# Nine norm factors by way of DRAM in place of TensorE products, in a two-layer hybrid decoder

## The chip, the cores and the metric

The kernel runs on one NeuronCore of a Trainium2 chip. The metric is the device time of one execution in microseconds (us), the median of several runs; lower is better. Beside the runs stands one profiled execution, whose trace gives every instruction's engine, start and duration.

The engines are TensorE (PE in the profile; PEld is its weight loading), VectorE (DVE), ScalarE (ACT), GpSimd (POOL) and SyncE (SP). Each takes its instructions strictly in the order in which the program has them, so an instruction that waits holds back all behind it on its engine. SP issues the weight loads; POOL issues the small transfers of this kernel.

## The reference, cut to what matters

Two layers on 256 positions of width 2048, batch 1, all in float32. The first layer mixes positions by a state-space model (SSD), the second by forgetting attention (FoX). Every branch begins and ends with an RMS norm.

```
def rmsnorm(x, w):
    y = x * rsqrt(mean(x * x, axis=-1) + EPS)        # one factor for each position
    return y * w

# end of the state-space mixer: 8 groups of 512 channels, each with a norm of its own
y  = y.reshape(b, l, 4096) * silu(z)
yg = y.reshape(b, l, 8, 512)
yg = yg * rsqrt(mean(yg * yg, axis=-1, keepdims=True) + EPS)
y  = yg.reshape(b, l, 4096) * norm_w
return y @ w_out

# the attention layer's first norm
proj = rmsnorm(h, norm_mix_pre[1]) @ fox_w_in       # q, k, v and the forget gates
```

A position's factor multiplies all channels of that position. The kernel holds activations with channels on the 128 partitions and the 256 positions along the free dimension (a tile is 128 x 256), so a factor has to be present on all 128 partitions, as a row of 256 numbers repeated 128 times.

## The kernel before

**Weights.** Every weight matrix is streamed once, in stages of up to 128 x 1024 numbers. For each stage SP loads a tile `raw` (six buffers), ScalarE casts it to a high part `wh` in the fast float32r format (L204), and VectorE subtracts to get a low part `wl` (L209); both have four buffers. TensorE then makes three products for each 128 x 128 block: weight high by activation high (L266), high by low (L267), low by high (L268). Stages are prepared two ahead of the one in use. A unit is one call of `unit`: a set of output columns over the whole contraction, here mostly 4 blocks of 128 columns in 8 stages of 24 products.

**Side work.** What else has to be done (transposes, small products, exponentials, scalings) stands in a queue of little tasks, `bg`; `unit` takes one task (sometimes two) from it after each stage's products. This sets the order of the program's text. A scheduler then orders each engine's instructions by its own estimate of when their operands will be ready, so an instruction can end up ahead of its place in the text. Where the text says `tc.issue_after` (and the helper `paced`, which ties an operation to the last low part), that order is kept.

**Norm factors.** `rstd_small` turns the sums of squares (a 128 x 256 tile of partial sums) into factors: four narrow products on TensorE (L349) put positions on partitions, VectorE makes mean plus epsilon (`ms`, L352), POOL takes the power -1/2 (`rs`, L355). `rs` is 128 x 2: position on the partition, half of the sequence in the column. `rstd_wide` spreads it: VectorE splits `rs` into high and low (`rh`, `rl`; L360, L361), TensorE makes four products with the identity as moving operand and the factor as broadcast weights (L365), ScalarE copies the result out of PSUM (L369). It is called 18 times in all.

**State-space stage (about 125 to 525 us).** For group g there is an xs unit (its outputs go through the convolution `conv_silu` into four tiles `xg`), the core tasks `core_tasks(g)` (decay matrices `E`, transposes of `xg` at L977 into `xd`, products of `E` and `xd` at L1018, then y), a z unit (y times the gate, sums of squares into `ssp`), and the gate tasks: `gn1` makes the small factor, `gn2` spreads it into `grw` (one buffer), `gn3` scales the group's four y tiles (L1055). The tasks of group g's norm run beside the xs unit of group g + 2. The last two groups' scalings are `paced` and stand among the tasks of the out-projection (`last7`). `ab`, the broadcast of the decays from DRAM, and the clearing of three columns of `xr` for each convolution are POOL's other work here.

**FoX layer (about 1480 us on).** The V part is five units with positions on the output partitions, so it needs only the small factor (`rsm`). `mk_r(False, rsm)` makes it, and spreads it into `rwide` for the q and k units; `rq` is `rwide` times the attention scale.

Of the kernel before, what the change touches and what calls it, by code (L numbers as in the profile page):

```python
# [7 lines left out]
F32 = mybir.dt.float32  # L8
# [6 lines left out]
P = 128  # L15
# [6 lines left out]
NG = 8  # L22
# [41 lines left out]
def tile_trunk(ctx, tc, a, out):  # L64
    nc = tc.nc
    mult, add, sub, mx_, mn_ = ALU.mult, ALU.add, ALU.subtract, ALU.max, ALU.min
    V, A, G, PE = nc.vector, nc.scalar, nc.gpsimd, nc.tensor

    def pool(stack, name, bufs=1, **kw):
        return stack.enter_context(tc.tile_pool(name=name, bufs=bufs, **kw))  # L70
# [10 lines left out]
    gap = pool(ctx, "gap")  # L81
    psa = pool(ctx, "psa", bufs=6, space=PSUM)
    psm = pool(ctx, "psm", bufs=2, space=PSUM)

    cnt = [0]

    def nm(s):
        cnt[0] += 1
        return f"{s}_{cnt[0]}"
# [268 lines left out]
    def rstd_wide(rs, o):  # L358
# [10 lines left out]
            mark[0] = A.copy(out=o, in_=ps[:, :T])  # L369
        return ps[:, :T]  # L370

    def log1p_exp_neg_abs(v, new):
        ab = new()
        V.scalar_tensor_tensor(out=ab, in0=v, scalar=-1.0, in1=v, op0=mult, op1=mx_)
        e = new()
        A.activation(e, ab, AF.Exp, scale=-1.0)
        d = ab
        V.tensor_scalar(out=d, in0=e, scalar1=2.0, scalar2=None, op0=add)
        r = new()
        V.reciprocal(out=r, in_=d)  # L380
        s = new()
        V.tensor_tensor(out=s, in0=e, in1=r, op=mult)
        q = r
        V.tensor_tensor(out=q, in0=s, in1=s, op=mult)
        pl = ab
        V.tensor_scalar(out=pl, in0=q, scalar1=1.0 / 13, scalar2=None, op0=mult)
        for k in (11, 9, 7, 5, 3):
            V.scalar_tensor_tensor(out=pl, in0=pl, scalar=1.0 / k, in1=q, op0=add, op1=mult)
        o = e
        V.scalar_tensor_tensor(out=o, in0=pl, scalar=1.0, in1=s, op0=add, op1=mult)  # L390
        return o
# [26 lines left out]
    rwide = cp.tile([P, T], F32, name="rwide")  # L418
# [122 lines left out]
    def mk_r(half=True, small=None):  # L541
        r = []

        def f1():
            r.append(rstd_small(ssb, D))
            if small is not None:
                V.tensor_copy(out=small, in_=r[0])

        def f2():
            rstd_wide(r[0], rwide)  # L550
            if half:
                V.tensor_scalar(out=rwide2, in0=rwide, scalar1=0.5, scalar2=None, op0=mult)
        return f1, f2
# [268 lines left out]
    with ExitStack() as ys:  # L822
        yp = pool(ys, "yp", side="right")
        y = [yp.tile([P, T], F32, name=f"y{c}") for c in range(32)]
        with ExitStack() as st:
# [136 lines left out]
            def core_tasks(g, xg):  # L962
                S = {}
                for q in range(2):
                    h0 = 8 * g + 4 * q
                    ab = s3[0].tile([P, 4, T], F32, tag="ab", name=nm("ab"), bufs=2)
                    G.dma_start(
                        out=ab.rearrange("p a n -> p (a n)"),
                        in_=acd[h0:h0 + 4, :].rearrange("h n -> (h n)").partition_broadcast(P))
                    S[f"a{q}"] = ab  # L970

                def xpose():
                    xd = S["xd"] = s3[0].tile([P, 2, 512], F32, tag="xd", name=nm("xd"), bufs=2)
                    ps = [misc(), misc()]

                    def turned(j, c):
                        return PE.transpose(out=ps[j][:, c * P:(c + 1) * P],  # L977
                                            in_=xg[c][:, j * P:(j + 1) * P], identity=ident)
                    joined(lambda: turned(0, 3),
                           [lambda j=j, c=c: turned(j, c) for j in range(2) for c in range(4)  # L980
                            if (j, c) != (0, 3)])
                    for j in range(2):
                        V.tensor_tensor(
                            out=xd[:, j, :].rearrange("p (h d) -> p h d", d=64),
                            in0=ps[j].rearrange("p (h d) -> p h d", d=64),
                            in1=dtk[:, j, 8 * g:8 * g + 8].unsqueeze(2).broadcast_to((P, 8, 64)),
                            op=mult)

                def decay(q, half):
                    h0 = 8 * g + 4 * q  # L990
                    ab = S[f"a{q}"]
                    if half == 0:
                        S[f"E{q}"] = s3[0].tile([P, 4, 384], F32, tag="E", name=nm("E"), bufs=2)
                    E = S[f"E{q}"]
                    with after(low_a[0]):
                        for i in range(2 * half, 2 * half + 2):
                            for b, lo in ((0, 0), (1, P), (2, P)):
                                A.activation(E[:, i, b * P:(b + 1) * P], ab[:, i, lo:lo + P],
                                             AF.Relu, scale=-1.0,
                                             bias=bias3[:, b, h0 + i:h0 + i + 1])  # L1000

                def decay2(q):
                    E = S[f"E{q}"]
                    with after(low_a[0]):
                        A.activation(E, E, AF.Exp, scale=-1.0)
                    V.tensor_tensor(out=E, in0=E,
                                    in1=cbm[g].unsqueeze(1).broadcast_to((P, 4, 384)),
                                    op=mult)

                def ymm_of(q):  # L1010
                    E, xd = S[f"E{q}"], S["xd"]
                    ps = S[f"p{q}"] = misc()

                    def mm(pr, s, b):
                        i = 2 * pr + s
                        hl = 4 * q + i
                        o = ps[s * 64:(s + 1) * 64, pr * T:(pr + 1) * T]
                        return PE.matmul(o[:, b * P:], lhsT=xd[:, b, hl * 64:(hl + 1) * 64],  # L1018
                                         rhs=E[:, i, b * T:(T, 384)[b]], start=b == 0,
                                         stop=b == 1)  # L1020
                    return [lambda pr=pr, s=s, b=b: mm(pr, s, b)
                            for pr in range(2) for b in range(2) for s in range(2)]

                def ymm():
                    todo = ymm_of(1) + ymm_of(0)
                    joined(todo[0], todo[1:])

                def y_of(q):
                    for pr in range(2):
                        c = 2 * q + pr  # L1030
                        V.scalar_tensor_tensor(out=y[4 * g + c], in0=xg[c],
                                               scalar=col("ssd_d", 4 * g + c),
                                               in1=S[f"p{q}"][:, pr * T:(pr + 1) * T],
                                               op0=mult, op1=add)

                def ymm_y():
                    ymm()
                    y_of(1)

                return [lambda: decay(0, 0), lambda: decay(0, 1), xpose, lambda: decay2(0),  # L1040
                        lambda: decay(1, 0), lambda: decay(1, 1), lambda: decay2(1), noop, ymm_y,
                        lambda: y_of(0), noop]

            def gate_tasks(g, S):
                def gn1():
                    S["rs"] = rstd_small(S["ss"], 512)

                def gn2():
                    S["rw"] = yp.tile([P, T], F32, tag="grw", name=nm("grw"), bufs=1)
                    rstd_wide(S["rs"], S["rw"])  # L1050

                def gn3():
                    for c in range(4):
                        yc = y[4 * g + c]
                        last_v[0] = V.scalar_tensor_tensor(out=yc, in0=yc, scalar=col("ssd_norm", 4 * g + c),  # L1055
                                               in1=S["rw"], op0=mult, op1=mult)
                if g < NG - 2:
                    return [noop, gn1, gn2, gn3]
                late.append(lambda: paced(gn3))
                return [noop, gn1, gn2] if g < NG - 1 else [gn1, noop, gn2, noop]  # L1060

            xgs, late, later, last7 = {}, [], [], []
            zt = {}

            def z_a(t):
# [87 lines left out]
                bg.append(lambda c=c: ysplit(c))  # L1153
            left[0] = 0
            z_unit(NG - 1, 2)
        xq_s = ExitStack()
        xq = pool(xq_s, "xq", bufs=16)
        zp = pool(xq_s, "zp")
        for t in range(4):
            acc, yc, ss = later[t]  # L1160
# [98 lines left out]
    for u in range(1, 5):  # L1259
        unit(lambda k: nxt[k], both if u == 1 else ev_v(u), tok=True,  # L1260
             late=(lambda: (drain(), v1()), v2) if u == 1 else ())
        if u == 1:
            V.tensor_scalar(out=rq, in0=rwide, scalar1=float(FOXS), scalar2=None, op0=mult)
    bg.extend((f1, noop, f2, noop, f3))
    ots = {}
# [178 lines left out]
```

## Time and profile before

| | |
|---|---|
| median of 3 runs | 2704.6 us (2704.22 to 2705.89) |
| profiled execution, its own time | 2704.73 us |
| its span, first to last instruction | 2702.9 us |
| TensorE busy | 2696.0 us |
| VectorE busy | 1782.5 us |
| ScalarE busy | 1398.9 us |
| POOL busy | 46.8 us |
| mean granted TensorE clock | 1.000 |
| weight loads (queue of SP) | 504.54 MB |

The span is what the instructions cover; the profiled execution's own time is 1.8 us more. Busy TensorE does not mean that it is at its peak, since matmuls overlap: what one costs is seen from the distance between starts. A row of the order of time gives the start, the duration, engine, line, operation, output tiles and input tiles, how many instructions of the kind followed each other, and in brackets how long the engine was idle before and who ended that. A row of a group gives count, busy time, mean duration and the idle time ahead.

### The profile page before, as it was taken

The numbers are of one execution on the slowest core, as the hardware profiler recorded it, in microseconds if no ns is written. First come the engines' busy times: TensorE is split into PE (matmuls) and PEld (weight loads), VectorE is DVE, ScalarE is ACT, GpSimd is POOL, SyncE is SP. The second block draws the span as 40 slices with busy tenths as digits, with TensorE's granted clock in tenths as the row PEclk, the third lists the DMA queues.
The fourth block names the chain that finished last, engine by engine and source line by source line (L and its number), as shares of the span: only waits on it lengthen the run. The fifth ranks groups of instructions, "written<-read, shape, count | busy, mean of one in ns | idle before, by whom it ended". The sixth has DMA issues, their size and how long they took to land. (4 is left out here: it accounts for less than half of the span.)

```text
span 2702.9 us, 56196 instructions
## 1 busy us (share of the span) xinstructions
PE 2696.0 (100%) x23302; PEld 2680.0 (99%) x23302; DVE 1782.5 (66%) x2747; ACT 1398.9 (52%) x2156; POOL 46.8 (2%) x108
## 2 busy tenths in 40 slices
PE   9999999999999999999999999999999999999999
PEld 9999999999999999999999999999999999999999
DVE  8788888754966545666568656656865545656577
ACT  6577666554644444444446544455644444444455
POOL 0000000000000000000000000000000000000000
PEclk9999999999999999999999999999999999999999
DMA  7666666565666666666656676655766666666655
GB/s 267 190 203 203 189 196 189 162 213 174 195 203 195 195 195 193 192 176 208 199 162 208 180 223 184 178 160 171 205 203 194 195 195 192 193 180 209 195 165 171
DMA packets 262736, 520.42 MB, mean 193 GB/s; under 512 B 17440, under 2 KB 44224, under 8 KB 262480
## 3 DMA queue, kind: packets, MB, share of 16 engines
q1 hardware_dynamic: 258784, 504.54, 62.2%
q0 software_dynamic: 3552, 12.15, 1.4%
q8 instruction: 182, 2.98, 0.5%
q14 instruction: 74, 0.61, 0.1%
q10 hardware_dynamic: 144, 0.14, 0.0%
HBM read 514.58 MB, written 2.18 MB: 191 GB/s over the span
## 5 line engine op out<-in xcount | busy, mean ns | idle before, releaser
L209 DVE TENSOR_TENSOR wl<-raw,wh 128x1024 fp32r<-128x1024 f32 (+4 forms) x1020 | 1174.2, 1153 | 751.9 <-ACT wh L204 750.5
L204 ACT CAST wh<-raw 128x1024 fp32r<-128x1024 f32 (+4 forms) x1020 | 1014.2, 997 | 1116.6 <-PE acc L267 985.0
L267 PE MATMUL acc<-x,wh 128*128 128x256 f32 x5120 | 1392.0, 277 | 0.0
L268 PE MATMUL acc<-x,wl 128*128 128x256 f32 x5120 | 1365.4, 276 | 0.0
L266 PE MATMUL acc<-x,wh 128*128 128x256 f32 x5120 | 1356.6, 277 | 0.1
L267 PEld LDWEIGHTS acc<-x,wh 128*128 128x128 f32 x5120 | 961.0, 188 | 2.0 <-issue 1.9
L268 PEld LDWEIGHTS acc<-x,wl 128*128 128x128 f32 x5120 | 948.2, 188 | 0.8 <-issue 0.7
L266 PEld LDWEIGHTS acc<-x,wh 128*128 128x128 f32 x5120 | 936.2, 188 | 1.4 <-issue 0.9
L267 PE MATMUL acc<-a,wh 128*128 128x256 f32 x1408 | 388.1, 276 | 0.0
L266 PE MATMUL acc<-a,wh 128*128 128x256 f32 x1408 | 388.0, 276 | 0.0
L268 PE MATMUL acc<-a,wl 128*128 128x256 f32 x1408 | 385.4, 275 | 0.0
L267 PEld LDWEIGHTS acc<-a,wh 128*128 128x128 f32 x1408 | 264.4, 188 | 0.0
L266 PEld LDWEIGHTS acc<-a,wh 128*128 128x128 f32 x1408 | 264.2, 188 | 0.0
L268 PEld LDWEIGHTS acc<-a,wl 128*128 128x128 f32 x1408 | 263.5, 188 | 0.0
L266 PE MATMUL acc<-xb,wh 128*128 128x256 f32 x512 | 143.8, 281 | 1.1 <-DVE qk L296 1.1
L267 PE MATMUL acc<-xb,wh 128*128 128x256 f32 x512 | 141.4, 276 | 0.0
L268 PE MATMUL acc<-xb,wl 128*128 128x256 f32 x512 | 140.6, 276 | 0.0
L266 PEld LDWEIGHTS acc<-xb,wh 128*128 128x128 f32 x512 | 96.1, 188 | 1.7 <-DVE qk L296 1.5
L267 PEld LDWEIGHTS acc<-xb,wh 128*128 128x128 f32 x512 | 96.2, 188 | 0.2
L268 PEld LDWEIGHTS acc<-xb,wl 128*128 128x128 f32 x512 | 95.8, 188 | 0.2 <-issue 0.2
L914 DVE SCALAR_TENSOR_TENSOR g<-xr,vec,g 128x256 f32<-128x256 f32 x144 | 66.5, 481 | 8.2 <-ACT g L911 7.6
L266 PE MATMUL acc<-xq,wh 128*128 128x256 f32 x256 | 70.7, 276 | 0.0
(217 smaller groups left out, 1984.4 us busy)
## 6 DMA issues: line engine op xcount, KB each, us to landing
raw<-down SPq DMA_DIRECT2D x176, 512.0 KB, 3.9
raw<-ssd_in SPq DMA_DIRECT2D x144, 512.0 KB, 4.1
raw<-gate SPq DMA_DIRECT2D x128, 512.0 KB, 3.7
raw<-up SPq DMA_DIRECT2D x128, 512.0 KB, 3.6
raw<-fox_in SPq DMA_DIRECT2D x64, 512.0 KB, 4.0
raw<-gate SPq DMA_DIRECT2D x64, 384.0 KB, 3.2
raw<-up SPq DMA_DIRECT2D x64, 384.0 KB, 3.5
raw<-ssd_out SPq DMA_DIRECT2D x40, 512.0 KB, 4.4
```

What stands on the lines that cost most here:

```text
L204: low_a[0] = A.copy(out=wh[:, :kc * n], in_=raw[:, :kc * n])
L209: low[0] = V.tensor_tensor(out=wl[:, :kc * n], in0=raw[:, :kc * n], in1=wh.bitcast(F32)[:, :kc * n], op=sub)
L266: PE.matmul(o, lhsT=w, rhs=x[:, 0, :], start=st, stop=False)
L267: PE.matmul(o, lhsT=w, rhs=x[:, 1, :], start=False, stop=False)
L268: last = PE.matmul(o, lhsT=wl[:, c, t * P:(t + 1) * P], rhs=x[:, 0, :], start=False, stop=sp)
L914: V.scalar_tensor_tensor(out=c, in0=xr[:, k:k + T], scalar=col(f"conv_w{k}", cc), in1=c, op0=mult, op1=add)
```

## The change

A new pool of DRAM tiles and a new helper `rstd_sent` stand beside `rstd_wide`. The helper writes `rs` from the partitions into 256 consecutive numbers in DRAM, and reads them back to all 128 partitions; both transfers are issued by POOL. It takes the place of `rstd_wide` in the eight group norms and in the FoX layer's first norm. `gn2` is gone; `gn1` now does both steps. For the first six groups `gn3` is put into a list `scale` and called from a later place of the task queue, where the core tasks had a `noop`. The eighth group's scaling comes one task later. `rq` is written behind the last V unit in place of the second.

```
+    rp = pool(ctx, "rp", space=bass.MemoryType.DRAM)
...
+    def rstd_sent(rs, o):
+        d = rp.tile([2, P], F32, tag="rsd", name=nm("rsd"), bufs=2)
+        G.dma_start(out=d.rearrange("j p -> p j"), in_=rs)
+        G.dma_start(out=o, in_=d.rearrange("j p -> (j p)").partition_broadcast(P))
...
         def f2():
-            rstd_wide(r[0], rwide)
+            (rstd_wide if half else rstd_sent)(r[0], rwide)
...
-                        lambda: decay(1, 0), lambda: decay(1, 1), lambda: decay2(1), noop, ymm_y,
+                        lambda: decay(1, 0), lambda: decay(1, 1), lambda: decay2(1), scale_y, ymm_y,
...
                 def gn1():
-                    S["rs"] = rstd_small(S["ss"], 512)
-
-                def gn2():
                     S["rw"] = yp.tile([P, T], F32, tag="grw", name=nm("grw"), bufs=1)
-                    rstd_wide(S["rs"], S["rw"])
+                    rstd_sent(rstd_small(S["ss"], 512), S["rw"])
...
                 if g < NG - 2:
-                    return [noop, gn1, gn2, gn3]
+                    return [noop, gn1, lambda: scale.append(gn3), noop]
                 late.append(lambda: paced(gn3))
-                return [noop, gn1, gn2] if g < NG - 1 else [gn1, noop, gn2, noop]
+                return [noop, gn1, noop] if g < NG - 1 else [gn1, noop, noop, noop, noop]
+
+            def scale_y():
+                if scale:
+                    scale.popleft()()
...
-        if u == 1:
+        if u == 4:
             V.tensor_scalar(out=rq, in0=rwide, scalar1=float(FOXS), scalar2=None, op0=mult)
```

What the scheduler makes of it, on VectorE around the scaling of the fourth group. Before (`wl` are low parts, `ms` the mean plus epsilon, `y` with `grw` the scaling, `xr` the evacuation of the next unit's outputs):

```order
L352 TENSOR_SCALAR ms_4797<-mi_4794 128x2
L209 TENSOR_TENSOR wl_4845<-raw_4842,wh_4844 128x1024
L360 CAST rh_4832<-rs_4799 128x2
L361 TENSOR_TENSOR rl_4833<-rs_4799,rh_4832 128x2
L209 TENSOR_TENSOR wl_4879<-raw_4876,wh_4878 128x1024
L1055 SCALAR_TENSOR_TENSOR y_193<-y_193,vec,grw_4831 128x256
L1055 SCALAR_TENSOR_TENSOR y_194<-y_194,vec,grw_4831 128x256
L1055 SCALAR_TENSOR_TENSOR y_195<-y_195,vec,grw_4831 128x256
L1055 SCALAR_TENSOR_TENSOR y_196<-y_196,vec,grw_4831 128x256
L296 TENSOR_TENSOR xr_4906<-acc_4618,rwide 128x256
L209 TENSOR_TENSOR wl_4961<-raw_4958,wh_4960 128x1024
```

and the same place now:

```order
L353 TENSOR_SCALAR ms_4779<-mi_4776 128x2
L210 TENSOR_TENSOR wl_4819<-raw_4816,wh_4818 128x1024
L210 TENSOR_TENSOR wl_4849<-raw_4846,wh_4848 128x1024
L1058 SCALAR_TENSOR_TENSOR y_195<-y_195,vec,grw_4775 128x256
L1058 SCALAR_TENSOR_TENSOR y_196<-y_196,vec,grw_4775 128x256
L1058 SCALAR_TENSOR_TENSOR y_197<-y_197,vec,grw_4775 128x256
L1058 SCALAR_TENSOR_TENSOR y_198<-y_198,vec,grw_4775 128x256
L297 TENSOR_TENSOR xr_4876<-acc_4599,rwide 128x256
L210 TENSOR_TENSOR wl_4931<-raw_4928,wh_4930 128x1024
```

The two small operations are gone; the scaling stands where it stood, two low parts behind `ms`, though its call in the text is some eight stages later. It is the same for the other five of the first six groups; in the first three, evacuations and convolution steps stand between `ms` and the scaling as well. On POOL at the same place, before (`rs` is the power, `ab` the broadcast of decays):

```order
L908 MEMSET xr_4906 128x3
L908 MEMSET xr_4917 128x3
L355 TENSOR_TENSOR rs_4799<-ms_4797,mhalf 128x2
L908 MEMSET xr_4928 128x3
L967 DMA ab_5611<-acd 128x1024
L908 MEMSET xr_4939 128x3
```

and now:

```order
L914 MEMSET xr_4876 128x3
L973 DMA ab_4922<-acd 128x1024
L914 MEMSET xr_4887 128x3
L356 TENSOR_TENSOR rs_4781<-ms_4779,mhalf 128x2
L375 DMA rsd_4783<-rs_4781 128x2x1
L376 DMA grw_4775<-rsd_4783 128x256
L914 MEMSET xr_4898 128x3
L973 DMA ab_5574<-acd 128x1024
```

The two new transfers stand directly behind the power, ahead of the clearing of the next `xr`; the second cannot be issued before the first has landed. On TensorE the 36 products are gone, and some of the state-space stage's own products stand elsewhere among the weight products: the eight transposes of the third group 20 products earlier, of the fourth 38 later, of the fifth 12 earlier, of the sixth and seventh 10 later, and the first product of E and xd of the fifth group 18 earlier. SP's queue is the same row for row.

More of the change, by code (lines that the diff above doesn't have):

```diff
@@ L1057, in gate_tasks @@
                 if g < NG - 2:
-                    return [noop, gn1, gn2, gn3]
+                    return [noop, gn1, lambda: scale.append(gn3), noop]
                 late.append(lambda: paced(gn3))
-                return [noop, gn1, gn2] if g < NG - 1 else [gn1, noop, gn2, noop]
-            xgs, late, later, last7 = {}, [], [], []
+                return [noop, gn1, noop] if g < NG - 1 else [gn1, noop, noop, noop, noop]
+            def scale_y():
+                if scale:
+                    scale.popleft()()
+            xgs, late, later, last7, scale = {}, [], [], [], deque()
             zt = {}
@@ L1155, in tile_trunk @@
             z_unit(NG - 1, 2)
+            assert not scale
         xq_s = ExitStack()
```

## The prediction

> **What bounds the kernel now.** I read the page's busy shares first, then the costliest groups, then the order of time on TensorE around one of the products that go.
>
> ```profile
> PE 2696.0 (100%) x23302; PEld 2680.0 (99%) x23302; DVE 1782.5 (66%) x2747; ACT 1398.9 (52%) x2156; POOL 46.8 (2%) x108
> L209 DVE TENSOR_TENSOR wl<-raw,wh 128x1024 fp32r<-128x1024 f32 (+4 forms) x1020 | 1174.2, 1153 | 751.9 <-ACT wh L204 750.5
> L204 ACT CAST wh<-raw 128x1024 fp32r<-128x1024 f32 (+4 forms) x1020 | 1014.2, 997 | 1116.6 <-PE acc L267 985.0
> ```
>
> TensorE is the bound from end to end: its matmuls leave 7 us of 2702.9 uncovered. VectorE's low parts (L209) wait for ScalarE's casts (L204), and those wait for TensorE to hand a weight buffer back. So work taken off TensorE shortens the span by itself, as long as VectorE and ScalarE keep their lead over it. The whole question is whether the new path costs them that lead.
>
> **What goes from TensorE.** Nine calls of `rstd_wide`, four 128-column products each, two of them in this group (all 18 calls) and two in one like it. One call in the order of time:
>
> ```profile
> L365 PE MATMUL mi<-identr,rh 128*128 128x128 f32 x36 | 9.1, 256 | 0.0
> ```
>
> ```profile
> 343.36 0.28 PE L266 MATMUL acc<-x,wh 128*128 128x256 f32 x1
> 343.47 0.28 PE L267 MATMUL acc<-x,wh 128*128 128x256 f32 x1
> 343.59 0.22 PE L365 MATMUL mi<-identr,rh 128*128 128x128 f32 x1
> 343.64 0.33 PE L268 MATMUL acc<-x,wl 128*128 128x256 f32 x1
> 343.81 0.22 PE L365 MATMUL mi<-identr,rl 128*128 128x128 f32 x1
> 343.88 0.27 PE L365 MATMUL mi<-identr,rh 128*128 128x128 f32 x1
> 343.98 0.28 PE L365 MATMUL mi<-identr,rl 128*128 128x128 f32 x1
> 344.10 0.33 PE L266 MATMUL acc<-x,wh 128*128 128x256 f32 x1
> 344.27 0.28 PE L267 MATMUL acc<-x,wh 128*128 128x256 f32 x1
> 344.39 0.28 PE L268 MATMUL acc<-x,wl 128*128 128x256 f32 x1
> ```
>
> Durations overlap, so the cost is read from starts. Undisturbed, one weight product follows the next after 0.113 us (344.27 to 344.39 is 0.12, rounded). From 343.36 to 344.39 five weight products start, worth 5 x 0.113 = 0.57; the stretch is 1.03. The four inserted products cost 0.46 us, including the longer gap that each neighbour shows. Nine times 0.46 is **4.1 us**, all of it on the bound. I take this for the whole possible gain. The nine pairs of tiny VectorE operations (L360, L361) and the nine ScalarE copies (L369) go too; I cost them at nothing, since neither engine is the bound.
>
> **What is added: a chain through DRAM.** POOL's power, a transfer of 256 numbers to DRAM, its landing, a second transfer that spreads them to 128 partitions, its landing. The trace has no such pair; the nearest rows:
>
> ```profile
> ab<-acd POOLq DMA_DIRECT2D x16, 512.0 KB, 5.3
> ck<-csd POOLq DMA_DIRECT2D x12, 256.0 KB, 6.1
> m<-pT POOLq DMA_DIRECT2D x4, 128.0 KB, 3.9
> acd<-acT POOLq DMA_DIRECT2D x1, 64.0 KB, 3.2
> fb<-fox_b POOLq DMA_DIRECT2D x1, 8.0 KB, 3.7
> csd<-csT POOLq DMA_DIRECT2D x1, 16.0 KB, 2.5
> ```
>
> ```profile
> 339.60 0.71 POOL L355 TENSOR_TENSOR rs<-ms,mhalf 128x2 f32<-128x2 f32 x1 [22.74 <-DVE ms L352]
> 351.36 0.09 POOL L908 MEMSET xr<- 128x3 f32 x1 [11.05 <-ACT E L998]
> 1596.68 0.55 POOL L1233 DMA_DIRECT2D csd<-csT  x1 [66.82 <-ACT csT L1232]
> 1599.47 0.79 POOL L1245 DMA_DIRECT2D ck<-csd  x1 [2.24 <-DMA csd<-csT]
> ```
>
> The write to DRAM is nearest to acd, also a write and in the same stage of the program: 3.2. Its bounds are 2.5 (csd, also a small write) and 6.1 (ck, the transfer cut into the most pieces). The spread is nearest to m<-pT, of the same 128 KB: 3.9; bounds 3.7 (fb) and 5.3 (ab). csd landed at 1599.18 and the transfer that needs it was issued at 1599.47, so the hand-over is 0.3. From the end of VectorE's `ms` to the factor in place: 0.1 + 0.7 + 0.1 + 3.2 + 0.3 + 3.9 + 0.1 = **8.4 us**, with 7.4 and 12.6 as ends.
>
> [...]
>
> POOL itself stands still between its two issues, some 3 us. Behind it are the clearings of `xr`; the next starts at 351.36, 11 us after the power ends, so they keep their time. I cost that at nothing; it stays free while the first transfer lands within some 10 us.
>
> **Where the result is waited for.** The text of the program puts a group's scaling nine stages later. The instruction order does not: for six of the eight groups the scaling stands on VectorE where it stood, two low parts behind `ms`, because the scheduler pulled it forward. Only the last two groups are pinned. Times of before, around the fourth group's scaling:
>
> ```profile
> 339.36 0.16 DVE L352 TENSOR_SCALAR ms<-mi 128x2 f32<-128x2 f32 x1 [0.86 <-PE mi L349]
> 343.22 1.23 DVE L209 TENSOR_TENSOR wl<-raw,wh 128x1024 fp32r<-128x1024 f32 x1 [1.69 <-ACT wh L204]
> 344.70 1.67 DVE L1055 SCALAR_TENSOR_TENSOR y<-y,vec,grw 128x256 f32<-128x256 f32 x4 [0.26 <-ACT grw L369]
> 346.30 0.42 DVE L296 TENSOR_TENSOR xr<-acc,rwide 128x256 f32<-128x256 f32 x1
> 346.63 1.22 DVE L209 TENSOR_TENSOR wl<-raw,wh 128x1024 fp32r<-128x1024 f32 x1
> 347.76 0.42 DVE L296 TENSOR_TENSOR xr<-acc,rwide 128x256 f32<-128x256 f32 x1
> ```
>
> `ms` ends at 339.52, so the factor is there at 347.9. VectorE reaches the scaling when the second low part ends, at 344.45, and stands for **3.5 us** with everything behind it: evacuations, low parts, convolutions. Six groups and the fox layer's `rq` (moved in the text to the last V unit, but in the order still two low parts behind `ms`) do this. It costs the span only where the lead is smaller. VectorE has little room to catch up after a scaling:
>
> ```profile
> 211.00:224.00 13.00, 11.76 (x17) 1.00 0.78 228
> 304.00:322.00 18.00, 17.27 (x26) 1.00 0.79 246
> 350.00:368.00 18.00, 16.98 (x25) 1.00 0.78 250
> ```
>
> ```profile
> L1006 DVE TENSOR_TENSOR E<-E,cbm 128x1536 f32<-128x1536 f32 x16 | 28.1, 1755 | 0.7 <-ACT E L1005 0.4
> L983 DVE TENSOR_TENSOR xd<-mi,rpe 128x512 f32<-128x512 f32 x16 | 10.8, 687 | 0.5 <-PE mi L977 0.5
> ```
>
> The first rows give stretch, length and VectorE's busy time, the others the mean of one operation in the state-space stage (125 to 525 us). So I run VectorE without a gap from the factor on, by starts: 0.40 for a short fused operation, 0.34 for an evacuation, 1.13 for a low part (346.63 to 347.76), 1.67 for the product with E and 0.6 for xd (their means less the 0.08 by which neighbours overlap), and compare with when TensorE needs the result:
>
> ```profile
> 201.60 0.16 DVE L352 TENSOR_SCALAR ms<-mi 128x2 f32<-128x2 f32 x1
> 224.10 1.04 PE L977 MATMUL mi<-cst,xg 128*128 128x128 f32 x8
> 293.38 0.16 DVE L352 TENSOR_SCALAR ms<-mi 128x2 f32<-128x2 f32 x1 [0.81 <-PE mi L349]
> 327.52 0.65 PE L1018 MATMUL mi<-E,xd 128*64 128x256 f32 x4
> 353.62 0.28 PE L268 MATMUL acc<-x,wl 128*128 128x256 f32 x1
> ```
>
> - First group. The transposes at 224.10 now stand 20 weight products earlier (2.27) and lack the four products (0.46): needed at 221.37. From scaling through the fourth `xg` VectorE has 13 short operations, one evacuation, four low parts, one E: 11.7. 201.76 + chain + 11.7 + 0.1 reaches 221.37 at a chain of 7.8. At 8.4 TensorE waits 0.6.
> - Third group. The products with xd at 327.52 stand 18 earlier: needed at 325.0. VectorE has 21 short operations, four evacuations, nine low parts, two E and two xd before them: 24.5. From 293.54 this holds up to a chain of 6.8. At 8.4 TensorE waits 1.6.
> - Fourth to sixth. Right behind the scaling stand an evacuation and a low part (3.1 with the scalings); by count its first product is the one at 353.62. That holds up to 10.5, and a later low part of the same unit, by the same count, up to 9.7.
> - Second group 9.6, fox layer 10.5, eighth group 11.2, all by the same count; the seventh never.
>
> At 8.4 the loss is 0.6 + 1.6 = **2.2 us**. Sum: -4.1 + 2.2 = -1.9. The profiled execution took 2704.73 with a span of 2702.9, so 2702.8 and a span of 2701.0; it is 0.1 over the median of 2704.6, which makes the forecast **2702.7**. At 7.4 the loss is 0.6 (2701.1); at 10.0 it is 2.2 + 0.4 + 3.2 + 3 x 0.3 = 6.7 (2707.2), and if VectorE's gaps in the three stretches above (1.2, 0.7, 1.0) return behind every wait, some 4 more (2711); at 12.6 about 26 (2726).
>
> **Rivals.**
> - *All hidden.* The factor comes within 6.8, or TensorE is not held at the two moved places. For it: the lead elsewhere is 9.6 and more. Against: both nearest rows together give 8.4. Result 2704.6 - 4.1 = 2700.5.
> - *Slower: the write in 4-byte pieces.* `rs` has two numbers in each partition and they lie 512 bytes apart in DRAM, so the first transfer is 256 pieces of 4 bytes, where every row above moves at least 64 in one. If it takes as long as ck (6.1), the chain is 11.3 and the loss by the same counts 3.5 + 1.7 + 4.5 + 3 x 1.6 + 0.8 + 0.1 = 15.4: 2716. It decides from a chain of about 10.5, where the loss passes 9.5. Against: csd and acd, small writes from POOL, took 2.5 and 3.2. [...]
> - *Faster by more than 0.2%* needs 5.4 us, 1.3 more than all nine sets cost by their starts. Nothing in the rows gives it.
>
> **Chances.** 0.2% (5.4 us) is about what a measurement of this kernel can tell from no change. Forecast, chain between 7 and 10.5: 0.55. All hidden: 0.18. Slow write: 0.22. More than the sum allows: 0.05. The first two lie within 0.2%, so faster 0.05, same 0.73, slower 0.22. The range goes from 2700, a little below all hidden, to 2711, the forecast's worst; the likeliest case alone spans 2701 to 2709.
>
> **What would show it.** Right: L365 at x18 in each of its two groups; VectorE's idle time before the scaling line some 3 us for each of six groups, ended by a transfer; the transposes or E products of the groups behind the first and third scaling with TensorE idle ahead of them; nothing after 1540 us changed. Wrong: the first transfer landing after 5 us or more, low parts that TensorE waits for in every group (slower), or a scaling that finds its factor in place (all hidden).

## The result, and the profile after

| | before | after |
|---|---|---|
| median | 2704.78 us (4 runs, 2704.22 to 2705.89) | 2770.77 us (4 runs, 2770.40 to 2773.08) |
| ratio | | 1.0247, 95% interval 1.0235 to 1.0259 |
| span of the profiled execution | 2702.9 us | 2768.7 us |
| mean granted TensorE clock | 1.000 | 0.989 |

The change made the kernel 66 us slower. The products that were to go are gone, 36 matmuls, but TensorE is no longer busy from end to end:

```profile
PE 2711.2 (98%) x23266; PEld 2693.4 (97%) x23266; DVE 1777.4 (64%) x2729; ACT 1393.7 (50%) x2147; POOL 58.8 (2%) x126
```

The waits say who held whom (engine, line, releaser, then total us, how often, longest). First VectorE's, then TensorE's:

```profile
DVE y L1058 <- DMA grw<-rsd: 71.9, 7, 11.3
DVE rq L1271 <- DMA rwide<-rsd: 9.0, 1, 9.0
```

```profile
PE acc L267 <- DVE xr L297: 25.4, 3, 8.8
PE acc L269 <- DVE wl L210: 16.6, 3, 6.0
PE acc L268 <- DVE x L312: 5.9, 1, 5.9
PE acc L262 <- DVE wl L210: 3.5, 1, 3.5
```

VectorE stands 81 us at the scalings and at `rq`, always for the second transfer. TensorE stops in eight places, and each releaser is a VectorE operation that stands behind a scaling in the queue: a low part (`wl`), an evacuation (`xr`), a split (`x`). The DMA rows name the transfer that came late (count, size, median us from issue to landing):

```profile
grw<-rsd POOLq DMA_DIRECT2D x8, 128.0 KB, 4.8
rsd<-rs POOLq DMA_DIRECT2D x9, 1.0 KB, 8.8
```

One kilobyte takes 8.8 us to land; the 128 KB behind it take 4.8. The fourth group in order of time, on POOL, VectorE and TensorE:

```profile
363.69 0.72 POOL L356 TENSOR_TENSOR rs<-ms,mhalf 128x2 f32<-128x2 f32 x1 [22.56 <-DVE ms L353]
364.71 0.76 POOL L375 DMA_DIRECT2D rsd<-rs  x1 [0.30 <-POOL rs L356]
374.73 0.57 POOL L376 DMA_DIRECT2D grw<-rsd  x1 [9.26 <-DMA rsd<-rs]
```

```profile
363.45 0.16 DVE L353 TENSOR_SCALAR ms<-mi 128x2 f32<-128x2 f32 x1 [0.86 <-PE mi L350]
367.26 1.23 DVE L210 TENSOR_TENSOR wl<-raw,wh 128x1024 fp32r<-128x1024 f32 x1 [1.91 <-ACT wh L205]
379.20 1.67 DVE L1058 SCALAR_TENSOR_TENSOR y<-y,vec,grw 128x256 f32<-128x256 f32 x4 [10.72 <-DMA grw<-rsd]
380.79 0.42 DVE L297 TENSOR_TENSOR xr<-acc,rwide 128x256 f32<-128x256 f32 x1
```

```profile
372.66 0.28 PE L268 MATMUL acc<-x,wh 128*128 128x256 f32 x1
372.77 0.28 PE L269 MATMUL acc<-x,wl 128*128 128x256 f32 x1
381.26 0.58 PE L267 MATMUL acc<-x,wh 128*128 128x256 f32 x1 [8.21 <-DVE xr L297]
381.64 0.41 PE L268 MATMUL acc<-x,wh 128*128 128x256 f32 x1
381.86 0.41 PE L269 MATMUL acc<-x,wl 128*128 128x256 f32 x1
```

`ms` ends at 363.61. The write is issued at 364.71, the read only at 374.73, the scaling starts at 379.20: 15.6 us in all. Right behind the scaling stands the evacuation `xr` at 380.79, which frees an accumulator, and TensorE, stopped since 372.77, goes on at 381.26. After that it isn't back at its pace: products start 0.21 us apart, not 0.11. The stretches show why (busy us and count of each engine, then granted clock, DMA share, GB/s):

```profile
372.50:381.50 9.00, 0.79 (x6) 0.59 (x6) 2.30 (x6) 0.26 (x1) 0.57 (x1) 0.68 0.40 96
381.50:386.00 4.50, 4.50 (x22) 4.50 (x23) 4.43 (x9) 4.20 (x11) 0.35 (x2) 0.51 0.50 127
386.00:400.00 14.00, 14.00 (x126) 14.00 (x126) 12.76 (x19) 13.60 (x25) 1.12 (x5) 1.00 0.76 242
```

For 4.5 us after the stop the granted clock is 0.51, and from 386 us on it is 1.00 again (the last experiment below shows which stops were followed by the half clock and which not).

The books close. The distances between starts at the eight stops are 5.77, 5.39, 6.26, 8.49, 9.09, 8.66, 6.13 (groups one to six and eight) and 3.86 us (attention layer's norm). Less one ordinary distance each (0.11, the last 0.19) they sum to 52.7. Products at half clock behind them start late by 17.5 in all (14.8 in the groups, 2.7 in the last). With 4.1 saved: 52.7 + 17.5 - 4.1 = +66.1; the spans differ by 65.8.

### The profile page after: what moved, and what is told of

The parts are those of the page before. It is cut to its first block, busy times and chain, and to the rows that moved or that the text cites. A ratio compares the mean times of both kernels' runs of the same rounds, so it can differ in the third digit from the quotient of the medians.

```text
span 2768.7 us, 56119 instructions
## 1 busy us (share of the span) xinstructions
PE 2711.2 (98%) x23266; PEld 2693.4 (97%) x23266; DVE 1777.4 (64%) x2729; ACT 1393.7 (50%) x2147; POOL 58.8 (2%) x126
## 4 chain that ended last, share of the span: by engine, by line
PE 78%; DMA 1%; DVE 0%; issue 0%; ACT 0%; POOL 0%; DVEq 0%; POOLq 0%
PE acc L267 24%; PE acc L268 24%; PE acc L269 24%; PE acc L262 1%; PE acc L263 1%; PE acc L261 1%; PE mi L1286 0%; PE mi L1334 0%; DMA rsd<-rs 0%; PE acc L458 0%; DMA ck<-csd 0%; PE acc L461 0%; PE acc L462 0%; PE mi L1318 0%; DMA rwide<-rsd 0%; PE mi L350 0%
## 5 line engine op out<-in xcount | busy, mean ns | idle before, releaser
L267 PE MATMUL acc<-xq,wh 128*128 128x256 f32 x256 | 70.7, 276 | 0.0
L268 PE MATMUL acc<-xq,wh 128*128 128x256 f32 x256 | 70.7, 276 | 0.0
```

The lines of the kernel that those rows point to most:

```text
L267: PE.matmul(o, lhsT=w, rhs=x[:, 0, :], start=st, stop=False)
L268: PE.matmul(o, lhsT=w, rhs=x[:, 1, :], start=False, stop=False)
```

## Experiments

Two questions: does the loss come from VectorE standing at a scaling that the scheduler pulled forward, or from the transfers as such? And why does one kilobyte need 8.8 us?

**The scaling put where the text has it.** The eighth group's factor comes from products again.

```
             def scale_y():
                 if scale:
-                    scale.popleft()()
+                    paced(scale.popleft())
...
         if u == 4:
-            V.tensor_scalar(out=rq, in0=rwide, scalar1=float(FOXS), scalar2=None, op0=mult)
+            with after(low[0]):
+                V.tensor_scalar(out=rq, in0=rwide, scalar1=float(FOXS), scalar2=None, op0=mult)
```

> The changed kernel with the scaling of each group's outputs, and the product rq, held behind the weight residuals of their place in the text, so that VectorE comes to a group's scaling nine residuals (some 30 us) after ms and no longer two to four; the eighth group has its factor from TensorE products, as before. Eight norms still go through DRAM in the same pieces. Theory 1 (the loss is VectorE standing at a scaling that was put ahead of the factor's arrival): no stop of TensorE there, 8 x 0.46 = 3.7 us saved, 2701.1 us (2700.0 to 2702.5). Theory 2 (the transfers themselves cost, by GpSimd's queue held or by traffic against the weights): most of the 66 us stays, 2740 to 2770 us. Theory 3 (the saved products shorten nothing, since another engine sets the pace there): 2704.8 us.

Measured: 2699.87 us (11 runs, 2698.72 to 2700.93) against 2704.22 (21 runs), ratio 0.9984 (0.9975 to 0.9993). It beats the changed kernel by 71 us and the one before by 4.35 us (0.16%). The write is as slow as ever, and nobody waits for it (POOL, then VectorE, fourth group, then the longest wait of TensorE that is left, which the changed kernel has too):

```profile
339.74 0.76 POOL L375 DMA_DIRECT2D rsd<-rs  x1 [0.30 <-POOL rs L356]
349.19 0.58 POOL L376 DMA_DIRECT2D grw<-rsd  x1 [8.69 <-DMA rsd<-rs]
```

```profile
365.69 1.22 DVE L210 TENSOR_TENSOR wl<-raw,wh 128x1024 fp32r<-128x1024 f32 x1
366.83 1.67 DVE L1063 SCALAR_TENSOR_TENSOR y<-y,vec,grw 128x256 f32<-128x256 f32 x4
```

```profile
PE mi L422 <- DVE mhalf L404: 1.1, 1, 1.1
```

The scaling now follows `ms` by 28 us, without a gap; in the other five of the first six groups by 20 to 28. So the whole loss was the wait; transfers, POOL's queue and the traffic cost nothing that can be measured here. The gain is 4.35 us where 3.7 was counted, which puts the median just below theory 1's range; the other 0.7 lies within the interval of the ratio (a gain of 1.9 to 6.8 us), and I did not trace it.

**One norm alone.** Only the attention layer's norm goes through DRAM; the groups are as before.

```
-            rstd_wide(r[0], rwide)
+            (rstd_wide if half else rstd_sent)(r[0], rwide)
...
-        if u == 1:
+        if u == 4:
```

> The kernel before with one of the nine norms changed: only the factor of the attention layer's norm goes through DRAM, and rq comes three units later in the text; the groups are as before. Theory 1 (each wait is paid by itself): the stop of 3.9 us that the changed kernel showed at this place, less 0.46 us of products, 2708.2 us (2707 to 2709.5), one wait of VectorE of about 9 us at rq. Theory 2 (the loss at this place came from the state in which the groups' stops had left the clock or the queues): no more than 1 us, 2704 to 2706 us.

Measured: 2709.88 us (11 runs, 2708.07 to 2713.38) against 2704.22, ratio 1.0022 (1.0014 to 1.0031): 5.7 slower, more than theory 1 gave. One wait of VectorE, one stop of TensorE, and the clock behind it:

```profile
DVE rq L1269 <- DMA rwide<-rsd: 9.6, 1, 9.6
```

```profile
PE acc L262 <- DVE wl L210: 4.1, 1, 4.1
```

```profile
1546.00:1549.60 3.60, 3.60 (x12) 3.48 (x12) 2.47 (x3) 0.08 (x1) 0.00 (x0) 0.54 0.78 222
```

The stop costs 4.3, eleven products at a clock of 0.54 cost another 1.7, and 0.46 is saved: 5.5. My expectation had left the clock out. Theory 2 falls: the wait costs by itself.

**Half the pieces.** In the groups `rsd` is written as 128 pieces of 8 bytes.

```
+        d = rp.tile([P, 2], F32, tag="rsp", name=nm("rsp"), bufs=2)
+        G.dma_start(out=d, in_=rs)
+        G.dma_start(out=o, in_=d.rearrange("p j -> (p j)").partition_broadcast(P))
...
-                                               in1=S["rw"], op0=mult, op1=mult)
+                                               in1=S["rw"].rearrange("p (q j) -> p j q", j=2),
+                                               op0=mult, op1=mult)
```

> The changed kernel with the groups' rsd written as 128 pieces of 8 bytes, a partition's two numbers side by side, and the scaling reading the broadcast row with a step of two; VectorE's order is that of the changed kernel, and the attention layer's norm keeps its 256 pieces of 4 bytes. Theory 1 (the time of the write goes with the number of pieces): the write lands after about 6 us in place of 9, each wait of VectorE is some 3 us shorter, and of the stops of TensorE (5 to 9 us each) 3 us each are gone at seven places, with some of the half-rate products after them: 2740 to 2752 us. Theory 2 (any small write through this queue lands after 8 to 10 us, however it is cut): the time of the changed kernel, 2768 to 2773 us. Theory 3 (only pieces of 4 bytes are slow): the write lands after 3 to 4 us, waits of 4 to 5 us remain, 2705 to 2715 us.

Measured: 2733.06 us (4 runs, 2729.50 to 2734.76) against 2704.22, ratio 1.0105 (1.0091 to 1.0118).

```profile
rsp<-rs POOLq DMA_DIRECT2D x8, 1.0 KB, 4.1
rsd<-rs POOLq DMA_DIRECT2D x1, 1.0 KB, 9.2
```

The same bytes through the same queue: 4.1 us as pieces of 8 bytes (the median; two of the eight took 5.5 and 7.0), 8.1 to 9.5 as pieces of 4 at the same eight places of the changed kernel, and 9.2 here in the one norm that kept 4. That speaks against theory 2. The time lies below theory 1's 2740 and above theory 3's 2715, so neither was right; the landing is nearly theory 3's.

**Forms of the write by themselves.** A chain of single transfers in a stretch where POOL is free.

```
+        forms = ((rows, b[:, :2], G),
+                 (one[0:256].rearrange("(p j) -> p j", j=2), b[:, :2], G),
...
+        for _ in range(2):
+            for o, i, e in forms:
+                e.dma_start(out=o, in_=i)
+                G.dma_start(out=b, in_=one[0:256].partition_broadcast(P))
```

> The kernel before, with a chain of small transfers added in the second half of the state-space layer's FFN, where GpSimd has nothing else to do. Each write to a DRAM tile is followed by the broadcast read of its first 256 numbers, and each waits for the one before, twice through a list: 256 numbers as 256 pieces of 4 bytes in the form of rstd_sent; as 128 pieces of 8 bytes; 128 pieces of 4 bytes; 32 pieces of 4 bytes; 256 pieces of 4 bytes, each 1 KB from the next; 128 pieces of 64, of 512 and of 1024 bytes; the first form again, issued by ScalarE; and 128 pieces of 8 bytes from SBUF to SBUF. Nothing is left out; only the landings are read, the time of the kernel isn't. Theory 1 (the small pieces are what is slow): the first form lands after 8 to 10 us, as the changed kernel's did; half the pieces after about half of the surplus over 3.2 us, so 128 pieces after 5 to 6.5 us and 32 pieces after 3 to 4; 512 and 1024 bytes after about 3.2 us, as the acd row did. Theory 2 (GpSimd's queue is slow in that stage of the changed kernel, whatever it carries): here, in another stage, all forms land after 2 to 4 us, the first one too. Theory 3 (neighbouring pieces that share a line of DRAM get in each other's way): the form with pieces 1 KB apart lands after 3 to 5 us, the first after 8 to 10. Theory 4 (the descriptors that GpSimd makes for so many pieces take the time): ScalarE's issue of the same form lands after 3 to 4 us.

Measured: the first form landed after 8.9 and 8.2 us, so theory 2 falls. ScalarE's issue of it took 8.7 and 8.2, so theory 4 falls. 128 pieces of 4 bytes took 10.7 and 8.4, as long as 256 of them, so between these two the count doesn't set it; 32 pieces took 4.2 and 3.5, so a small count does help, about as theory 1 has it. 128 pieces of 8 bytes took 6.9 and 5.5. The form from SBUF to SBUF took about 4.2 and 5.7 and is not used below. Pieces 1 KB apart, and all wide ones, took 1.7 to 2.0; but those rows were no fair comparison, as two stretches show:

```profile
1040.00:1050.70 10.70, 10.70 (x97) 10.70 (x96) 4.72 (x5) 4.21 (x4) 0.55 (x1) 1.00 0.85 109
1066.90:1068.80 1.90, 0.00 (x0) 0.00 (x0) 0.00 (x0) 0.00 (x0) 0.67 (x1) 0.66 0.02 1
```

In the second, ScalarE was already waiting for its own transfer in the chain, casts stood still, weights too, and nothing else moved (DMA share 0.02). Inconclusive on theory 3, hence a second probe.

> The first probe made clean: there the wide pieces fell into a time in which ScalarE waited and no weights moved, so its forms can't be compared. Now every form is issued by GpSimd at least once while the weights stream (first half of the chain) and once while ScalarE waits for the chain's end and they stand still (second half). Forms: 256 pieces of 4 bytes side by side (two rows of 512 bytes, as rstd_sent writes), the same 1 KB apart, 128 pieces of 4 bytes, 128 pieces of 8 bytes side by side and 2 KB apart, 128 pieces of 64, 512 and 1024 bytes. Nothing is left out; only landings and the bytes moved meanwhile are read. Theory 1 (the pieces alone cost): 256 pieces of 4 bytes land after 8 to 9 us with the weights and without them. Theory 2 (only with the weights' traffic: small writes and weight reads hold each other up): 8 to 9 us with the weights, 2 us without them; 64 bytes and more land after 2 to 4 us even with the weights. Theory 3 (any write waits for the traffic, whatever its pieces): all forms land after 5 to 9 us with the weights. Theory 4 (pieces of one line of DRAM get in each other's way): 1 KB or 2 KB apart they land in half the time, with the weights too.

| form | with the weights, us | weights at rest, us |
|---|---|---|
| 256 x 4 bytes, side by side | 9.0, 8.3 | 7.6, 8.1 |
| 256 x 4 bytes, 1 KB apart | 3.3, 3.8 | 2.0, 2.0 |
| 128 x 4 bytes, side by side | 10.7 | 7.3, 7.1 |
| 128 x 8 bytes, side by side | 4.3, 4.8 | 3.0, 3.3 |
| 128 x 8 bytes, 2 KB apart | 4.9, 4.9 | 1.7 |
| 128 x 64 bytes | 3.6, 3.5 | 1.7 |
| 128 x 512 bytes | 3.6 | 1.8 |
| 128 x 1024 bytes | 3.7, 4.0 | 2.0 |

Two pairs of rows on POOL, each a write and the read that waits for it (the bracket is POOL's idle time). The first pair is side by side, the second 1 KB apart, both with the weights at rest:

```profile
1160.89 0.72 POOL L391 DMA_DIRECT2D pd<-pb  x1 [3.21 <-DMA pb<-pd]
1168.76 0.55 POOL L392 DMA_DIRECT2D pb<-pd  x1 [7.14 <-DMA pd<-pb]
1173.60 0.68 POOL L391 DMA_DIRECT2D pd<-pb  x1 [4.29 <-DMA pb<-pd]
1175.84 0.55 POOL L392 DMA_DIRECT2D pb<-pd  x1 [1.56 <-DMA pd<-pb]
```

Theory 4 holds for pieces of 4 bytes: the same 256 pieces, moved apart, land like wide ones. For pieces of 8 bytes it holds only with the weights at rest (1.7 against 3.0 and 3.3). Theory 1 holds in so far as the weights' traffic is not what makes the touching pieces slow; the traffic adds 1 to 2 us to most forms, less to the slow one (0.2 to 1.4), and some 3 to two others. Theories 2 and 3 fall. The traffic suffers in turn: while the slow form was under way with the weights, all queues together moved 99 GB/s, and in a stretch with pieces of 8 bytes, 2 KB apart, 285:

```profile
1027.88:1036.88 9.00, 9.00 (x81) 9.00 (x81) 4.07 (x4) 3.85 (x6) 0.73 (x1) 1.00 0.81 99
1043.92:1048.77 4.85, 4.85 (x45) 4.85 (x44) 2.45 (x2) 1.74 (x2) 0.54 (x1) 1.00 0.88 285
```

How far apart is enough? The same chain, with nothing changed but the distance of the 256 pieces of 4 bytes:

> The second probe again, with the distance between the 256 pieces of 4 bytes as the only thing that changes: 8, 16, 32, 64, 128, 256, 512 and 1024 bytes, and the form of rstd_sent, once while the weights stream and once while they stand still. Nothing is left out; only landings are read. Theory 1 (pieces within one line of 64 bytes wait for each other): from 64 bytes on all land after 2 us without the weights, below it the time falls with the pieces in a line: 8 bytes apart 4 to 5, 32 bytes apart 2.5. Theory 2 (a line of 512 bytes): 2 us only from 512 bytes on, 64 bytes apart 2.7 (8 pieces to a line). Theory 3 (it is the 256 pieces spread over one DRAM page or bank): no distance below 1 KB is as fast as 1 KB.

Measured with the weights: 5.2 us at 8 bytes, 4.9 at 16, 4.3 at 32, 2.8 to 4.0 from 64 on, 8.8 side by side. With the weights at rest: 2.1 at 16 bytes, 1.9 from 32 on, 7.9 side by side; at 8 bytes the weights were still moving (5.7). The reads that wait for the write, at 16 bytes and side by side, both with the weights at rest:

```profile
1122.78 0.55 POOL L387 DMA_DIRECT2D pb<-pd  x1 [1.67 <-DMA pd<-pb]
1169.37 0.55 POOL L387 DMA_DIRECT2D pb<-pd  x1 [7.51 <-DMA pd<-pb]
```

None of the three theories is met: at 16 and 32 bytes several pieces lie within 64 bytes of each other, and at rest they land in 2 us. What makes pieces of 4 bytes that touch each other slow stays open.

**The same in place.** The changed kernel, pieces 1 KB apart, the scaling left where the scheduler had pulled it. What it leaves out is the right read: the transfer back still takes 256 numbers in a row, so the factor that arrives is not the norm's. A read that gathers the scattered pieces was not measured.

```
+        if not far:
+            far.append(rp.tile([P, 512], F32, name="rsf"))
+            G.dma_start(out=far[0], in_=cst[:, 0:512])
-        G.dma_start(out=d.rearrange("j p -> p j"), in_=rs)
-        G.dma_start(out=o, in_=d.rearrange("j p -> (j p)").partition_broadcast(P))
+        G.dma_start(out=far[0][:, 0:512:256], in_=rs)
+        G.dma_start(out=o, in_=far[0].rearrange("p n -> (p n)")[0:256].partition_broadcast(P))
```

> The changed kernel, all nine norms through DRAM and VectorE's order as there, but the 256 numbers of a norm are written 1 KB apart in one DRAM tile that is filled once at the start. The read is left as it is, 1 KB from the tile's beginning, so the factor that arrives is not the norm's: only the time of the way is right. Theory 1 (the write is slow because its pieces lie side by side): it lands after 3.3 to 3.8 us in place of 8.1 to 9.5, the way from ms to the scaling takes 9.5 to 10.3 us in place of 14.2 to 16.5, and the stop of TensorE at rq is gone. By the prediction's own count of lost time (2.2 us at 8.4, 6.7 to 11 at 10.0) that gives 2705 to 2711 us; by the kernel with pieces of 8 bytes (2733 us, of it 6 at rq, its way 0.7 us longer at seven places) 2718 to 2723 us. Theory 2 (in place it is the traffic or the stage, not where the pieces lie): the write lands after 6 to 9 us, 2750 to 2771 us.

Measured: 2704.28 us (10 runs, 2702.70 to 2706.92) against 2704.03 (13 runs), ratio 1.0000 (0.9990 to 1.0009). The landings, what is left of VectorE's wait, and TensorE's:

```profile
grw<-rsf POOLq DMA_DIRECT2D x8, 128.0 KB, 4.0
rsf<-rs POOLq DMA_DIRECT2D x9, 1.0 KB, 3.5
```

```profile
DVE y L1062 <- DMA grw<-rsf: 24.2, 7, 4.8
```

```profile
PE acc L267 <- DVE xr L297: 3.1, 3, 2.3
PE mi L987 <- DVE xg L928: 2.3, 2, 1.3
```

One property of one transfer takes 66 us out, so theory 2 falls. The way from `ms` to the scaling is 7.8 to 9.8 us in the seven groups that wait. At these ways the prediction's own count gives 1.5 us lost behind the first group (9.3, limit 7.8) and 3.0 behind the third (9.8, limit 6.8), so 2704.03 - 4.1 + 4.5 = 2704.4. That it meets the median to 0.1 us is partly luck: in the profiled execution, the slowest of the ten (2706.92), TensorE stood 1.4 and 1.2 us at these two places, but also 2.4, 0.5 and 0.7 us in groups four to six, where the count has nothing, and ran at half clock once. My scaling down from the kernel with 8-byte pieces, 2718 to 2723, was wrong: the ways became 1.2 to 3.5 us shorter in place of 0.7, since the read landed earlier too (4.0, there 5.0).

One stop in this kernel lasts 2.5 us, and behind it the granted clock is 0.50; in the kernel with 8-byte pieces one of 3.6 us, 463.10 to 466.70, leaves it at 1.00. The traces show where the two differ. In the trace of the changed kernel the changes of the granted clock lie on a grid of 3.41 us: the half-clock stretches behind the eight stops last 6.83 us (seven) and 10.24 (one), and the full ones between the first six groups 40.96, 47.79 or 51.20. The steps of this grid around the two stops, first the far pieces, then the 8-byte ones:

```profile
348.85:352.26 3.41, 1.34 (x12) 1.14 (x11) 1.87 (x5) 0.00 (x1) 0.00 (x0) 1.00 0.09 35
352.26:355.67 3.41, 3.22 (x15) 3.22 (x16) 3.38 (x6) 3.24 (x9) 0.00 (x0) 0.50 0.26 50
```

```profile
461.69:465.10 3.41, 1.67 (x15) 1.48 (x14) 0.44 (x2) 2.09 (x8) 0.00 (x0) 1.00 0.64 215
465.10:468.51 3.41, 1.79 (x15) 1.79 (x16) 3.41 (x8) 1.81 (x3) 0.00 (x0) 1.00 0.00 0
468.51:471.92 3.41, 3.41 (x32) 3.41 (x31) 3.38 (x7) 3.41 (x7) 0.10 (x1) 1.00 0.66 169
```

The shorter stop falls mostly into one step, in which TensorE is idle for 2.07 us, and the next step has half the clock. The longer one is cut in two by a grid line, with 1.74 and 1.62 us idle, and the step behind it has the full clock. In the changed kernel every step at full clock with 2.39 us idle or more was followed by a half-clock step, and none with 1.78 us or less. So besides the length of a stop it mattered here where it fell on the grid. The same program does not halve the clock every time: of the ten executions of this kernel three show a mean granted clock of 0.999, the profiled one among them, and seven 1.000.

## Why the prediction was wrong

**The step that failed** is "The write to DRAM is nearest to acd, also a write and in the same stage of the program: 3.2". It landed after 8.1 to 9.5 us. The row was chosen for kind, stage and bytes; the prediction saw that `rsd` is cut into pieces of 4 bytes, but took that for a rival and sized it by ck, 6.1, a transfer *from* DRAM. The probes show that no row of before bounded it: none writes touching pieces of 4 bytes. The upper end given for the chain, 12.6, was below every way that was waited for (14.2 to 16.5 us). (By the prediction's own terms the ends add up to 7.5 and 12.7, and the third group's limit to 6.9 in place of 6.8; this changes nothing.)

**The other terms of the chain** were small misses: issue of the write 1.1 us after `ms` (0.9), hand-over 0.3 to 0.55 (0.3), read 4.2 to 5.7, median 4.8 in the groups (3.9). With a write of 3.5 us, in place, the way is 9.0 on average, 8.4 was forecast, and the kernel takes 2704.28 against a forecast of 2702.7. So the one step brings the miss about, and the half clock below adds to it.

**Where TensorE begins to wait** was predicted as a length of the way for each place. Way minus stop gives the measured one. It is the same within 0.2 us in each kernel that stops there, where a place has several stops with their sum; for the first and third group it is read in the kernel with far pieces, since after the change a low part stops TensorE there first (at 10.0 and 10.4):

| place | predicted | measured |
|---|---|---|
| first group (transposes) | 7.8 | 7.9 |
| second group | 9.6 | 9.7 |
| third group (predicted at xd products) | 6.8 | 8.7, at transposes |
| fourth to sixth | 9.7 | 7.2 |
| eighth | 11.2 | 9.8 |
| attention layer | 10.5 | 10.6 |

The fourth to sixth are the wrong ones that matter: 15.6 - 8.4, 16.2 - 9.0 and 15.8 - 8.6 after, and 9.6 - 2.4 with the far pieces, are all 7.2. The prediction counted the low part behind the scaling; what holds is the evacuation ahead of it, whose accumulator TensorE's next product needs. Errors of both signs cancel: at the measured ways the predicted table gives 49.8 us of stops, measured were 52.7. So with the ways as they were measured, the prediction's own count would have given about 2750 us.

**Not priced at all**: products at half clock after each stop, 17.5 us of the 66, which is most of what is left between 2750 and 2771.

**Right**: 4.1 us saved on TensorE (the kernel with the scaling pinned gained 4.35, interval 1.9 to 6.8, with eight norms of nine); the scheduler pulls six scalings forward, and that decides; the seventh never waits; POOL's wait between its issues costs nothing.

**The rivals.** "Slower: the write in 4-byte pieces" is what happened, with the right place and sign, and a chance of 0.22. Its size was not: way 11.3 and 2716, against 15.7 (median) and 2771. Its reason holds only in part: with the weights at rest 256 pieces of 4 bytes take 2.0 us when they lie 1 KB apart, wide ones 1.7 to 2.0. Of these, 128 pieces of 64 bytes land in 1.7 us and of 512 bytes in 1.8, so the smaller size alone did not cost here. "All hidden", 2700.5, is about the time of the pinned kernel, 2699.87, but there a later scaling hides the chain, not a short one.

## What to carry to other kernels

When an order is decided by a scheduler, a result that now comes later must be given its place by force; written later in the text it was still waited for, and forcing it was worth 71 us here (with one norm of nine put back). Before a small transfer is put on such a way, look at how its pieces lie in DRAM, not at its bytes: 128 or 256 pieces of 4 bytes that touch those of other partitions took 7 to 11 us to land, 256 of them 64 bytes or more apart took 2 to 4 (what reading them back costs was not measured). When a stop of the bound engine is priced, subtract the length of the way that its queue can absorb (here a constant of each place), and add the products at half clock where the clock halves behind it, 1.4 to 2.9 us for each of the eight stops of the changed kernel.

## What was not expected of the hardware

- 256 pieces of 4 bytes side by side land in DRAM after 7.6 to 8.1 us with the weights at rest, 16 bytes apart after 2.1.
- While such a write is under way, the other queues slow down: 99 GB/s in all in the stretch of the second probe above, and in the changed kernel some 2 KB packets of weights, 84 ns each as a rule, took up to 8.4 us during the groups' writes, at most 2.2 us at other times. In the pinned kernel, whose writes are as slow, this cost no time: its longest wait of TensorE is the 1.1 us that the changed kernel has too.
- Behind a stop of TensorE of 2.5 us the granted clock was 0.50 for 3.4 us; behind one of 3.6 us, spread over two steps of the 3.41 us grid, it stayed at 1.00.
